# A hybrid decoder layer: one more weight block multiplied in seven products, and the gated DRAM transfers spread thinner over more jobs

## The chip, the cores and the metric

One core of a Trainium2 chip runs one launch of the kernel. The metric is the device time of that launch in microseconds (us); the lower, the better. Each kernel is executed several times, and the median is compared.

## The reference

One layer over 512 tokens (S) with a model width of 1024 (D), everything in float32:

```python
h = rmsnorm(x, norm_mix_g)
bg, cg, xv, q, k, v, z, a, b, ga, gb = split(h @ w_in)
y_a = (bg * causal_dwconv(cg * xv, conv_a_w)) @ w_a_out
y_b = gdn_branch(q, k, v, z, a, b, ...) @ w_b_out        # gated DeltaNet, 8 heads of 128
x = x + (sigmoid(ga) * y_a + sigmoid(gb) * y_b) @ w_o
h = rmsnorm(x, norm_ffn_g)
gate, val = split(causal_dwconv(h @ w_up, ffn_conv_w))   # 2 x 2816 columns
x = x + (silu(gate) * val) @ w_down
return rmsnorm(x, norm_final_g)
```

## The kernel before

**Jobs.** Every large matrix product is cut into jobs, and each job has one weight block of 1 MB: 16 tiles of 128x128, which make 256 output columns. `run_jobs` (L216) walks a list of 93 jobs. Job i's matmuls run while the block of job i+1 is split and the blocks of later jobs are loaded. The order is: jobs 0 to 15 make K, Q, V and Z of the DeltaNet branch; jobs 16 to 19 the gate GB; jobs 20 to 31 the convolution phase, four groups of CG, XV, BG; jobs 32 to 35 the gate GA; 36 to 39 `w_a_out` and 40 to 43 `w_b_out`; 44 to 50 `w_o`; 51 to 72 `w_up`; 73 to 92 `w_down`.

**Splitting.** A float32 weight is multiplied as a pair: `wh`, a rounded copy that ScalarE (ACT) makes at L150, and the rest `wl`, which VectorE (DVE) makes at L151. Three matmuls, wh by low part, wl by high part, wh by high part, stand for one exact product (`mm3`, L117). `wh` and `wl` have 12 buffers each (`WQ`). TensorE (PE) runs all of a job's matmuls from L109.

**Plain jobs and seven-product jobs.** A plain job (`col_job`, L249) splits 4 pieces and runs 48 matmuls of 512 columns. A seven-product job (`sum_job`, L308) uses a Strassen-like scheme over halves of the output columns, the depth and the tokens: 7 products of 12 matmuls of 256 columns, 84 matmuls in all. For that, its block (`SumBlock`, L165) makes sums of the weight quarters in place in the loaded buffer with four DVE instructions (L173), and splits 7 pieces instead of 4. The products run in the order 11, 12, s3, s2, s4, 22, s1. ACT copies partial results out of PSUM between them (`u` at L346 and L351, `v` at L349 and L353): product s2 writes the same PSUM bank that L346 reads, and so waits for it. Two DVE additions (L335, L339) then assemble the output, and the job's own use of it (`consume`) follows. In the convolution phase, all jobs but XV1 (job 24) are seven-product jobs. For them, half of `hT` is copied into a layout of its own (`hk`, `beside`, L305) by four transfers of POOL's DMA queue at the start of the phase.

**Loads.** There are two raw buffers. Block i+2 goes into the buffer of block i when the splits of block i are done. From job 21 on (`FINE`) a block is loaded in four quarters on SP's queue (L145, L206). Engines run ahead of PE: a load leaves as soon as its buffer is free.

**DRAM sums.** The products with `w_o` and `w_down` use sums of weight quarters too, made in DRAM by transfers on POOL's software queue: plain copies, and copies that add to what is there (`Sums.form`, L180, L1188). They are 112 transfers of 256 KB: first 32 for `w_o` (8 copies, 8 adding, 4 copies, 4 adding, 4 copies, 4 adding), then 80 for `w_down` in the same six steps (20, 20, 10, 10, 10, 10). They are handed out by `feed` (L235), which job i calls for block i+2: POOL copies one element of that block's raw buffer (the "gate copy", L237), which waits until the second quarter of the block has landed, and then issues the next few transfers. Gate copies and transfers are kept in program order on POOL. Everything else is ordered per engine by a scheduler at compile time, by readiness as it estimates it.

Before the change a gated job issues `FEED` = 3 transfers. The list is filled in `open_conv` (L1219), when job 20 starts, so the first gate copy is that of job 21. The `w_o` blocks (44 to 50) and the first two of `w_up` (51, 52) have no gate. The last of the 112 transfers goes out in job 67. `w_o`'s own sums are first loaded for job 44.

POOL also computes the small powers of the norms: `fac` (L1034) for the last heads of the DeltaNet branch, which ends in jobs 18 and 19, and `r` (L1450) in the norm ahead of `w_up`, which ends in jobs 48 to 50.

Of the kernel before, what the change touches and what calls it, by code (L numbers as in the profile page):

```python
# [26 lines left out]
C_BG, C_CG, C_XV, C_Q, C_K, C_V, C_Z, C_GA, C_GB = range(0, 36, 4)  # L27
# [2 lines left out]
Y_F = (5, 4, 6, 3)  # L30
WARM = 3
WQ = 12
FEED = 3
FINE = 21
Y_M = 10

# [25 lines left out]
def layer_kernel(ctx, tc, x, norm_mix_g, w_in, w_ab, conv_a_w, gdn_conv_w, gdn_A_log, gdn_dt_bias,  # L62
# [25 lines left out]
    def advance(queue, n):  # L88
        while n and queue:
            queue[0].step()  # L90
            if queue[0].done:
                queue.popleft()
            else:
                n -= 1
# [38 lines left out]
    class Block:  # L133
        def __init__(self, src, quarter=(4, P)):
            self.src, self.quarter = src, quarter
            self.raw, self.ready, self.lead, self.fed, self.fine = None, False, 2, True, False
            self.wh, self.wl = {}, {}

        def load(self):
# [55 lines left out]
    class FormBlock(Block):  # L195
        def __init__(self, runs, names, lead, place):
            super().__init__(None, (S,))
            self.runs, self.names, self.lead, self.place, self.fed = runs, names, lead, place, False

        def load(self):  # L200
            if self.raw is not None:
# [14 lines left out]
    def run_jobs(jobs):  # L216
        for block, _ in jobs[FINE:]:
            block.fine = True
        jobs[1][0].load()
        for i, (block, use) in enumerate(jobs):  # L220
            Task(block.split()).finish()
            drain(splits)
            if i + 1 < len(jobs):
                splits.append(Task(jobs[i + 1][0].split()))
            for j, (later, _) in enumerate(jobs[i + 2:i + 5]):
                if later.lead >= j + 2:
                    later.load()
            if adds and i + 2 < len(jobs) and jobs[i + 2][0].fed:
                feed(jobs[i + 2][0].raw)
            use(block.wh, block.wl)  # L230


    gate = const.tile([1, 64], F32, name="gate")

    def feed(raw):  # L235
        el = raw[0:1, 1]
        tc.keep_in_program_order(pool.tensor_copy(out=gate[:, 0:1], in_=el[:, 0:1]))  # L237
        advance(adds, FEED)


    def piece(w, j, k):
# [7 lines left out]
    def col_job(w, i, xs, consume, pre=None):  # L249
        def use(wh, wl):  # L250
            if pre:
                pre()
            x_ = xs() if callable(xs) else xs
            for j in range(GW // P):
                o = bank()
                products(o, wh, wl, j, x_)
                evacs.append(Task(consume(j, o)))
        return Block(lambda: w[i]), use
# [49 lines left out]
    def sum_job(w, i, xs, sums, consume, place, pre=None, uv=None, near=lambda: None):  # L308
        def use(wh, wl):
            if pre:  # L310
                pre()
            drain(sums_of)
            x_, ts, low = xs() if callable(xs) else xs, sums(), near()
            A, B, C = bank(), bank(), bank()
            L, R = slice(0, HS), slice(HS, S)
            dst = place()
            u, v = uv() if uv else (scratch("u"), scratch("v"))

            def times(o, form, b, first):
                mm3(o, [(wh[form][:, k], wl[form][:, k], b[0][:, k], b[1][:, k]) for k in range(ND // 2)],  # L320
                    first, not first)

            def quarter(K, T):
                if K and low:
                    return [low[e][T] for e in range(2)]
                return [x_[e][:, K * 4:K * 4 + 4, T * HS:T * HS + HS] for e in range(2)]

            def t(i_):
                return [ts[e][i_] for e in range(2)]

            d = dst.rearrange("p (j t c) -> p t j c", j=2, t=2)
            pair = lambda a: a.rearrange("p (j c) -> p j c", j=2)

            def firsts():
                dve.tensor_tensor(out=d[:, 0], in0=pair(B), in1=pair(u), op=ALU.add)  # L335
                yield

            def seconds():
                dve.tensor_tensor(out=d[:, 1], in0=A[:, L].unsqueeze(1).broadcast_to([P, 2, HS]), in1=pair(v),  # L339
                                  op=ALU.add)  # L340
                yield
                for j in range(2):
                    yield from consume(j, dst[:, j * S:(j + 1) * S])

            times(A[:, L], "11", quarter(0, 0), True)
            act.copy(out=u[:, L], in_=A[:, L])  # L346
            times(B[:, L], "12", quarter(1, 0), True)
            times(B[:, R], "s3", t(2), False)
            act.copy(out=v[:, R], in_=B[:, R])  # L349
            times(A[:, L], "s2", t(1), False)  # L350
            act.copy(out=u[:, R], in_=A[:, L])  # L351
            times(C[:, L], "s4", quarter(1, 1), True)
            act.copy(out=v[:, L], in_=C[:, L])  # L353
            times(B[:, R], "22", t(3), False)
            evacs.append(Task(firsts()))
            times(A[:, L], "s1", t(0), False)
            evacs.append(Task(seconds()))
        return SumBlock(lambda: w[i]), use
# [751 lines left out]
    jobs = []  # L1110
# [12 lines left out]
    def gb_use(g):  # L1123
        def c(j, o):
            act.activation(out=gb()[:, 2 * g + j, :], in_=o, func=AF.Sigmoid)
            yield
        return c

    def gb_place(g):
        return lambda: gb()[:, 2 * g:2 * g + 2, :].rearrange("p k n -> p (k n)")  # L1130
# [18 lines left out]
    uv = lambda: cvs  # L1149
    for g in range(4):  # L1150
        if g == 0:
            jobs.append(col_job(w_in, C_GB + g, hT, gb_use(g)))
        else:
            jobs.append(sum_job(w_in, C_GB + g, hT, hsums, gb_use(g), gb_place(g), uv=uv))


    st = {}
# [46 lines left out]
            return [(0, LAST, self.last)], [("v4", e) for e in range(LAST)]  # L1204

    down_w = Sums("d", w_down, (0, 1, 2, 3, 4, 5, 7, 8, 9, 10))
    EIGHT = 6
    o_w = Sums("o", w_o, (0, 1, 2, 3))

    def open_conv():  # L1210
        drain(evacs)
        drain(chains)
        drain(mids)
        drain(backs)
        p2.close()
        sc = st["sc"] = p3.enter_context(tc.tile_pool(name="sc", bufs=1, side="right"))
        st["ya"] = Rows([by_columns(page(n, "ya")) for n in ("kq1", "CT")])
        room["pool"] = sc
        adds.extend((Task(o_w.form()), Task(down_w.form())))  # L1219
        st["near"] = beside(hT, [[by_columns(t, HS) for t in halves_of(page(n, "hk", F32R, UP))] for n in ("KU1", "AV1")])  # L1220

    def open_mix():
# [16 lines left out]
    def xv_c(g):  # L1239
        def c(j, o):  # L1240
            m = 2 * g + j
            u = held[g][:, j * S:(j + 1) * S]
            dve.tensor_tensor(out=u, in0=o, in1=u, op=ALU.mult)
            c_ = tmp("c", 2)
            yield from conv(c_, u, ca_w(m), 3)
            held["c", m] = c_
        return c
# [9 lines left out]
    for g in range(4):  # L1257
        jobs += [sum_job(w_in, C_CG + g, hT, hsums, nothing, cg_place(g), None if g else open_conv,
                         near=near if g else lambda: None),
                 sum_job(w_in, C_XV + g, hT, hsums, xv_c(g), pair_out, near=near) if g != 1 else  # L1260
                 col_job(w_in, C_XV + g, hT, xv_c(g)),
                 sum_job(w_in, C_BG + g, hT, hsums, bg_c(g), pair_out, near=near)]

    def ga_c(g):
# [234 lines left out]
    def o_top(q):  # L1499
        def use(wh, wl):  # L1500
            for tau in range(2):
                for i in range(2):
                    times_b(o_banks, *mix_b(2 * q + i), FORMS_T, tau, wh, wl, i, q + i == 0, q + i == 2)
                if q == 1:
                    fin1(tau, [o_banks["11"][tau], o_banks["22"][tau]])
        return use
# [4 lines left out]
    jobs += [(FormBlock(*o_w.first_pass(p), 2, raw), o_first(p)) for p in range(ND // 2)]  # L1511
    jobs.append((FormBlock(*o_w.low(), 2, raw), o_low))
    jobs += [(FormBlock(*o_w.top(q), 2, raw), o_top(q)) for q in range(2)]


    gates = {}
# [72 lines left out]
    for g in range(NF // 2):  # L1589
        def up_job(i, c, plain, pre=None):  # L1590
            if plain:
                return col_job(w_up, i, lambda: st["h2"], c, pre)
            return sum_job(w_up, i, lambda: st["h2"], hsums, c, pair_out, pre,
                           near=near if 2 < i < NA // 2 + 1 or NF // 2 <= i < NF // 2 + NA // 2 else lambda: None)

        last = g == NF // 2 - 1
        gj = up_job(g, gate_c(g), g < 2 or last, (lambda: splits.append(prep_d(prep_a, 0))) if last else
                    start_near if g == 2 else None)
        vj = up_job(NF // 2 + g, val_c(g), g not in (4, 7))
        gj[0].fed = vj[0].fed = g > 0  # L1600
        jobs += [(gj[0], first_gate), (vj[0], first_val)] if g == 0 else [gj, vj]


# [216 lines left out]
```

## Time and profile before

| what | value |
|---|---|
| median of 3 executions | 948.6 us (947.57, 948.6, 950.33) |
| the profiled execution | 950.23 us |
| its span, first to last instruction | 948.5 us |
| mean granted TensorE clock | 0.996 |
| instructions | 17675 |
| gate copies on POOL (L237) | 38 |
| bytes read from and written to HBM | 133.64 MB, 32.78 MB |

The sums below are made against the profiled execution. "Busy" rows give the time in which an engine works and what share of the span that is; a row of a window "A:B" gives the same for the stretch from A to B us, with the number of instructions behind x, the granted clock, the busy share of the DMA engines and GB/s. A row of a group gives line, engine, operation, tiles (out<-in), count, busy time, mean ns of one, and behind the second bar the idle time of the engine just before these instructions with what ended it.

### The profile page before, as it was taken

To read this page: it belongs to the slowest core of one execution; us is meant where nothing else is said; L and a number is where in the kernel's file an instruction comes from. 1 tells how busy PE (TensorE), PEld (TensorE's weight loads), DVE (VectorE), ACT (ScalarE), POOL (GpSimd) and SP (SyncE) were. 2 spreads that over 40 slices of the span, in tenths; PEclk is the share of its full clock that TensorE was granted. 3 is DMA by queue.
4 is the path that set the end of the run, shared out by engine and by line. 5 is a ranking of instruction groups with operands and counts; after the bars stand their busy time and mean duration, and the time that the engine had idled before them with its cause. 6 is when DMAs were issued, how large, how long until landed. Compare 5 with 4: busy or idle time off the path is not lost. (4 is left out here: it accounts for less than half of the span.)

```text
span 948.5 us, 17675 instructions
## 1 busy us (share of the span) xinstructions
PE 933.4 (98%) x6512; PEld 824.5 (87%) x6512; DVE 779.5 (82%) x1448; ACT 547.0 (58%) x1202; POOL 176.5 (19%) x288
## 2 busy tenths in 40 slices
PE   8999999999999999999999999999999989999996
PEld 7888887987889999999888888988899988888885
DVE  6978686898968998999653679999999979969885
ACT  7895756576565654555632346466575556556563
POOL 3330401304111122221322000322314110000000
PEclk9999999999999999999999999999999999999999
DMA  6443312223023677867988355667976765077332
GB/s 231 157 142 103 116 54 90 76 63 89 9 91 90 197 178 160 209 170 179 295 203 179 89 176 199 164 172 223 231 177 203 155 133 173 6 276 251 107 100 89
DMA packets 82903, 142.42 MB, mean 150 GB/s; under 512 B 24795, under 2 KB 29824, under 8 KB 80256
## 3 DMA queue, kind: packets, MB, share of 16 engines
q1 hardware_dynamic: 65904, 107.47, 35.0%
q0 software_dynamic: 16768, 33.56, 18.2%
q8 instruction: 51, 0.84, 0.4%
q14 instruction: 36, 0.29, 0.1%
q10 hardware_dynamic: 144, 0.26, 0.1%
HBM read 133.64 MB, written 32.78 MB: 175 GB/s over the span
## 5 line engine op out<-in xcount | busy, mean ns | idle before, releaser
L150 ACT CAST wh<-raw 128x512 fp32r<-128x512 f32 x377 | 223.1, 620 | 189.6 <-PE ps L109 115.6
L151 DVE TENSOR_TENSOR wl<-raw,wh 128x512 fp32r<-128x512 f32 x377 | 250.7, 686 | 35.0 <-ACT wh L150 32.4
L109 PE MATMUL ps<-hT,wh 128*128 128x512 f32 (+1 forms) x888 | 251.7, 360 | 0.3 <-DVE hT L582 0.3
L109 PEld LDWEIGHTS ps<-hT,wh 128*128 128x128 f32 x888 | 156.9, 189 | 20.7 <-DVE hT L582 0.5
L109 PE MATMUL ps<-hT,wl 128*128 128x512 f32 (+1 forms) x444 | 152.2, 353 | 0.0
L109 PE MATMUL ps<-h,wh 128*128 128x512 f32 (+1 forms) x592 | 150.5, 341 | 0.0
L109 PEld LDWEIGHTS ps<-h,wh 128*128 128x128 f32 x592 | 103.5, 190 | 12.5
L109 PE MATMUL ps<-ts,wh 128*128 128x256 f32 x544 | 101.0, 279 | 1.5 <-ACT u L346 1.5
L109 PE MATMUL ps<-wh,xs 128*128 128x512 f32 (+1 forms) x320 | 96.7, 384 | 0.0
L109 PE MATMUL ps<-h,wl 128*128 128x512 f32 (+1 forms) x296 | 96.2, 341 | 0.0
L109 PEld LDWEIGHTS ps<-hT,wl 128*128 128x128 f32 x444 | 83.8, 189 | 9.8
L109 PEld LDWEIGHTS ps<-ts,wh 128*128 128x128 f32 x544 | 85.1, 188 | 2.2 <-ACT u L346 1.9
L173 DVE TENSOR_TENSOR raw<-raw 128x512 f32<-128x512 f32 x108 | 74.2, 687 | 3.2 <-POOL gate L237 1.2
L109 PEld LDWEIGHTS ps<-wh,xs 128*128 128x128 f32 x320 | 59.6, 188 | 11.8
L109 PE MATMUL ps<-ts,wl 128*128 128x256 f32 x272 | 65.5, 277 | 0.0
L109 PE MATMUL ps<-us,wh 128*128 128x256 f32 x320 | 59.3, 280 | 2.7 <-ACT u L346 2.7
L109 PEld LDWEIGHTS ps<-h,wl 128*128 128x128 f32 x296 | 56.2, 190 | 6.3
L109 PE MATMUL ps<-wl,xs 128*128 128x512 f32 (+1 forms) x160 | 61.4, 384 | 0.0
L237 POOL COPY gate<-raw 1x1 f32<-1x1 f32 x38 | 20.8, 546 | 207.5 <-DMA raw<-in_w_in_dram 74.4
L375 DVE SCALAR_TENSOR_TENSOR ct<-ps,wA,ct 128x511 f32<-128x511 f32 (+2 forms) x72 | 53.2, 741 | 4.0 <-ACT ct L372 3.8
L150 ACT CAST wh<-raws 128x512 fp32r<-128x512 f32 x66 | 39.5, 620 | 25.7 <-PE ps L109 8.6
L109 PEld LDWEIGHTS ps<-us,wh 128*128 128x128 f32 x320 | 50.7, 191 | 2.9 <-ACT u L346 2.9
(346 smaller groups left out, 1787.0 us busy)
## 6 DMA issues: line engine op xcount, KB each, us to landing
raw<-in_w_up_dram SPq DMA_DIRECT2D x88, 256.0 KB, 4.9
raw<-in_w_in_dram SPq DMA_DIRECT2D x20, 1024.0 KB, 5.2
raw<-in_w_in_dram SPq DMA_DIRECT2D x64, 256.0 KB, 4.7
dv<-in_w_down_dram POOLq DMA_DIRECT2D x50, 256.0 KB, 6.3
raws<-in_w_down_dram SPq DMA_DIRECT2D x32, 256.0 KB, 4.2
raws<-dv SPq DMA_DIRECT2D x24, 256.0 KB, 5.3
ov<-in_w_o_dram POOLq DMA_DIRECT2D x20, 256.0 KB, 6.1
raw<-in_w_a_out_dram SPq DMA_DIRECT2D x16, 256.0 KB, 5.7
```

The costliest lines, as they stand in the source:

```text
L109: pe.matmul(o, lhsT=a, rhs=b, start=start, stop=stop, skip_group_check=free)
L150: act.copy(out=wh, in_=src)
L151: dve.tensor_tensor(out=wl, in0=src, in1=wh.bitcast(F32), op=ALU.subtract)
L173: dve.tensor_tensor(out=r[q], in0=a, in1=b, op=op)
L237: tc.keep_in_program_order(pool.tensor_copy(out=gate[:, 0:1], in_=el[:, 0:1]))
L375: dve.scalar_tensor_tensor(out=dst[:, sh:], in0=src[:, :S - sh], scalar=wcol(j), in1=dst[:, sh:], op0=ALU.mult, op1=ALU.add)
```

## The change

1. XV1, the last plain job of the convolution phase (job 24), becomes a seven-product job like its neighbours.
2. A gated job issues two transfers (`FEED` = 2) instead of three. The 15 jobs whose blocks are 36 to 50 (`w_a_out`, `w_b_out`, `w_o`) get three (`FEED_MORE`); so the seven blocks of `w_o`, which had no gate, now have one.
3. The list is filled at the start of job 17 (GB1) instead of job 20 (CG0), so that jobs 18, 19 and 20 issue transfers too.

Counted out in the order of the jobs: jobs 18 to 33 issue 2 each (32, just the sums of `w_o`), jobs 34 to 48 issue 3 each (45), jobs 49 and 50 none, jobs 51 to 67 issue 2 each (34) and job 68 the last one. That is 49 gate copies instead of 38. The transfers themselves, their number, bytes and order, are the same.

```diff
-FEED = 3
+FEED = 2
+FEED_MORE = 3
...
-            self.raw, self.ready, self.lead, self.fed, self.fine = None, False, 2, True, False
+            self.raw, self.ready, self.lead, self.fed, self.fine = None, False, 2, FEED, False
...
-            self.runs, self.names, self.lead, self.place, self.fed = runs, names, lead, place, False
+            self.runs, self.names, self.lead, self.place, self.fed = runs, names, lead, place, 0
...
             if adds and i + 2 < len(jobs) and jobs[i + 2][0].fed:
-                feed(jobs[i + 2][0].raw)
+                feed(jobs[i + 2][0].raw, jobs[i + 2][0].fed)
...
-    def feed(raw):
+    def feed(raw, n):
         el = raw[0:1, 1]
         tc.keep_in_program_order(pool.tensor_copy(out=gate[:, 0:1], in_=el[:, 0:1]))
-        advance(adds, FEED)
+        advance(adds, n)
...
-            jobs.append(sum_job(w_in, C_GB + g, hT, hsums, gb_use(g), gb_place(g), uv=uv))
+            jobs.append(sum_job(w_in, C_GB + g, hT, hsums, gb_use(g), gb_place(g), (lambda: start_adds()) if g == 1 else None, uv=uv))
...
+    def start_adds():
+        adds.extend((Task(o_w.form()), Task(down_w.form())))
...
-        adds.extend((Task(o_w.form()), Task(down_w.form())))
...
-                 sum_job(w_in, C_XV + g, hT, hsums, xv_c(g), pair_out, near=near) if g != 1 else
-                 col_job(w_in, C_XV + g, hT, xv_c(g)),
+                 sum_job(w_in, C_XV + g, hT, hsums, xv_c(g), pair_out, near=near),
...
+    for block, _ in jobs[-15:]:
+        block.fed = FEED_MORE
...
-        gj[0].fed = vj[0].fed = g > 0
+        if g == 0:
+            gj[0].fed = vj[0].fed = 0
```

## The prediction

> **What bounds the kernel now.** I read the page's busy times first.
>
> ```profile
> PE 933.4 (98%) x6512; PEld 824.5 (87%) x6512; DVE 779.5 (82%) x1448; ACT 547.0 (58%) x1202; POOL 176.5 (19%) x288
> ```
>
> PE is the bound over the whole span, so an edit gains only by taking matmul time away or by closing one of PE's few pauses, and loses by opening one. Next come windows cut where jobs begin on PE: XV1, BG1, XV2, BG3, GA0, GA1, GA2.
>
> ```profile
> 351.90:362.80 10.90, 10.90 (x51) 9.02 (x50) 9.56 (x17) 3.91 (x8) 1.86 (x4) 1.00 0.94 221
> 362.80:372.40 9.60, 9.60 (x86) 9.60 (x84) 8.00 (x13) 5.72 (x12) 2.19 (x3) 1.00 0.84 158
> ...
> 382.00:391.60 9.60, 9.60 (x87) 9.60 (x85) 8.95 (x15) 5.03 (x11) 2.44 (x4) 1.00 0.66 216
> ...
> 420.40:430.00 9.60, 9.60 (x87) 9.60 (x85) 9.50 (x16) 4.24 (x10) 2.60 (x4) 1.00 0.70 170
> 430.00:440.00 10.00, 10.00 (x87) 9.86 (x86) 9.75 (x16) 5.13 (x11) 1.80 (x4) 1.00 0.72 195
> 440.00:450.60 10.60, 10.20 (x86) 9.99 (x85) 10.17 (x17) 8.02 (x18) 2.07 (x4) 1.00 0.65 176
> 450.60:461.70 11.10, 10.04 (x86) 9.85 (x85) 5.99 (x11) 8.24 (x19) 4.06 (x8) 1.00 0.94 306
> ```
>
> The columns are PE, PEld, DVE, ACT, POOL. A plain job takes 10.90 us, a seven-product job 9.60. DVE has 8.0 of 9.6 us to do right after the plain job, 9.5 by BG3: it falls behind over a row of seven-product jobs. By GA0 to GA2 PE needs 10.0, 10.6 and 11.1 us for a 9.6 us job: 2.9 us lost. The waits of that stretch (430 to 462 us) name the link:
>
> ```profile
> PEld ps L109 <- ACT u L346: 1.9, 2, 1.3
> ...
> ACT mixa L1266 <- DVE mixa L339: 0.8, 1, 0.8
> ```
>
> PE waits for the copy `u`, which stands in ACT's queue behind work that waits for DVE. That is the way a late DVE reaches PE.
>
> The last view is the chain that ended last, with windows around it (end of val 7, then gate 8 of `w_up`, job 67, from 767.0 to 781.4).
>
> ```profile
> 758.31 0.60 DVE o L339
> 758.91 0.60 DVE raw L173
> 759.51 0.60 DVE wl L151
> ...
> 763.36 0.61 DVE raw L173
> 763.97 0.02 SPq L145
> 764.00 0.03 issue
> 764.03 8.50 DMA raw<-in_w_up_dram
> ...
> 772.60 0.62 ACT wh L150
> 773.22 0.62 ACT v L372
> 773.84 0.27 ACT u L346
> ```
>
> ```profile
> 757.30:767.00 9.70, 9.70 (x86) 9.70 (x85) 8.96 (x15) 7.58 (x16) 2.71 (x4) 1.00 0.69 94
> 767.00:776.90 9.90, 7.20 (x51) 7.00 (x51) 5.54 (x10) 3.64 (x7) 1.01 (x2) 0.86 0.77 216
> 776.90:781.40 4.50, 4.50 (x38) 4.50 (x38) 4.43 (x8) 1.09 (x4) 0.00 (x0) 0.93 0.40 27
> ```
>
> Job 67 takes 14.4 us instead of 9.6: 4.8 us lost in one place, the largest pause of the run. A quarter of a later block was loaded in 8.50 us; ACT, in order, waited for it with the copy `u` of job 67 behind. `u` ended at 774.1. PE could have used it after three of its seven products, at 767.0 + 3/7 x 9.6 = 771.1, so 3.0 us are the pause. The clock rows (0.86 over 9.9 us, 0.93 over 4.5 us) give 1.4 + 0.3 = 1.7 us of lost clock: together 4.7.
>
> Why was the load slow? The median quarter of this weight takes 4.9 us, and three adding transfers were under way:
>
> ```profile
> raw<-in_w_up_dram SPq DMA_DIRECT2D x88, 256.0 KB, 4.9
> ```
>
> ```profile
> 758.05 2.54 POOL L1188 DMA_DIRECT2D dl<-in_w_down_dram  x3 [0.37 <-issue]
> ```
>
> ```profile
> DMA to landing us min/median/max: 7.3/9.2/11.3
> ```
>
> The last row is that of these three alone. Issued about 0.5 us apart from 758.05, they land near 765.4, 767.8 and 770.4, one every 2.5 us. The load, issued at 764.03, shared the DMA engines with two of them.
>
> **The change part by part.**
>
> *XV1 in seven products.* PE: 10.90 to 9.60, a gain of 1.3 us. DVE gets three more L151, four L173, one L335 and one L339: nine instructions at 0.60 us (the chain shows all three kinds at that spacing), 5.4 us. With the job 1.3 us shorter DVE stands 6.7 us later against PE. ACT gets three casts and four copies at about 0.6 and 0.4 us, 3.4 us, and has room (3.91 of 10.90 busy). What covers the 6.7 us is DVE's idle time from XV1 to GA0, of which these groups have all that counts:
>
> ```profile
> L151 DVE TENSOR_TENSOR wl<-raw,wh 128x512 fp32r<-128x512 f32 x58 | 38.6, 687 | 4.3 <-ACT wh L150 3.4
> L173 DVE TENSOR_TENSOR raw<-raw 128x512 f32<-128x512 f32 x33 | 22.7, 688 | 0.7
> ...
> L1243 DVE TENSOR_TENSOR o<-ps,o 128x512 f32<-128x512 f32 x2 | 1.4, 688 | 1.1 <-PE ps L109 1.1
> ```
>
> That is 4.3 + 0.7 + 1.1 = 6.1 us in 351.9 to 440. Most of the first figure is DVE waiting for a cast that ACT could not make because PE still held the `wh` buffers; a later DVE no longer waits for that. If all of it fills, 0.6 us are left over; some turn-around from L173 to cast to L151 stays, so I take 1.2 us. It comes out at GA1, where no slack is left. XV1 nets -1.3 + 1.2 = -0.1 us. Ends: -1.3 (no pause grows) and -1.3 + 6.7 = +5.4 (no idle time fills).
>
> *Earlier start: six copies in jobs 18 to 20.* POOL's queue there:
>
> ```profile
> 299.99 0.78 POOL L305 DMA_DIRECT2D hk<-hT  x1 [3.71 <-issue]
> 301.41 2.03 POOL L1034 TENSOR_TENSOR fac<-fac,nhalf 128x8 f32<-128x8 f32 x1 [0.64 <-DVE fac L1033]
> 309.59 0.78 POOL L305 DMA_DIRECT2D hk<-hT  x1 [6.15 <-PE ps L765]
> 316.37 0.76 POOL L305 DMA_DIRECT2D hk<-hT  x1 [6.00 <-issue]
> 324.17 0.18 POOL L237 COPY gate<-raw 1x1 f32<-1x1 f32 x1 [7.04 <-DVE raw L173]
> 324.71 1.64 POOL L1188 DMA_DIRECT2D ov<-in_w_o_dram  x3 [0.37 <-issue]
> ```
>
> A gate copy with two copies takes 0.18 + 0.37 + 2 x 0.55 = 1.6 us of POOL. The scheduler already moved `hk` ahead of `fac`, so it may do so with job 19's gate. Then `fac` starts at 300.8 + 1.6 + 0.2 = 302.6 instead of 301.4, and behind it wait, in turn, DVE's scaling by `fac`, L339 of GB2, ACT's sigmoid and the copy `u` of GB3:
>
> ```profile
> 305.85 0.35 ACT L346 COPY ct<-ps 128x256 f32<-128x256 f32 x1
> ```
>
> ```profile
> 302.50:313.20 10.70, 10.70 (x95) 10.70 (x94) 9.61 (x22) 6.18 (x13) 1.72 (x2) 1.00 0.36 100
> ```
>
> The copy ends at 306.2. The window is GB3's, so PE needs it after three of seven products, at 302.5 + 4.1 = 306.6. So 1.2 - 0.4 = 0.8 us if the gate goes first, 0 if not; I take 0.3. `hk` costs nothing: XV0 begins three jobs of 9.6 us before XV1, at 323.1, and reads the quarter that the last transfer brings in its fifth product, at 328.6; issued at 316.4 + 1.6 and even 6.0 us in flight (the wait behind the one before), it is there at 324.8. The cover is gone if the gate's own load comes over 3.8 us late, and then it costs what is late.
>
> *Two instead of three in jobs 21 to 33 and 51 to 66.* In the first stretch PE waits for no load, so this gains nothing. In the second it takes the third adding transfer out of the pile-up ahead of job 67. If the engines serve one thing after another, the load lands 2.5 us sooner, at 770.0, and 1.6 us of ACT work later PE has `u` at 771.6: a pause of 0.5. If load and transfers share half and half, it lands 1.25 sooner and the pause is 1.8. Nearer to the first: landings 2.5 us apart look like one after the other. I take 0.6 and no lost clock: 4.7 to 0.6, a gain of 4.1. Ends: 4.7 and 0 (the load comes late anyway). The Trainium skill ("DMA: Bandwidth & Descriptors", Queues, rings and completion order) says that each DMA engine goes round between the queues that have work, packet by packet; by that the pause of 1.8 would be right. No row here shows the turns.
>
> *Three each for `w_o`, 21 transfers in jobs 42 to 48.* POOL has been idle for long when the norm's power comes:
>
> ```profile
> 589.96 0.86 POOL L1450 TENSOR_TENSOR r<-r,nhalf 128x1 f32<-128x1 f32 x1 [77.41 <-ACT hn L1446]
> ```
>
> Loads run ahead of PE, and the last of these blocks is split before 587; with its gate at some 580 and 2.5 us for three transfers POOL is free 7 us early. Cost 0; without that cover up to 2.5 us, on the way to `w_up`. A wait of DVE for a gate copy (L173 rewrites what it reads) costs nothing either while DVE is ahead.
>
> *Last transfers in jobs 67 and 68.* Three late ones instead of one: 0, or job 67's pause again one job on.
>
> Sum on the profiled execution: 950.2 - 0.1 + 0.3 - 4.1 = 946.3. It was 1.6 us above the median of its three runs. No run shows whether the median one has the pause in full; I take half: 946.3 - 0.8 = 945.5.
>
> **Rivals.**
>
> (1) *The pause stays, or moves.* ACT's order is fixed before the run, and a cast needed 20 us later still stands ahead of `u`. For it: eight quarters and the transfers crowd together whatever the third does. Against it: the load needs to be only 3 us faster, and 4.9 is usual. Median 948.6 - 0.1 + 0.3 = 948.8.
>
> (2) *Shared engines*: load and transfers halve the engines, the pause is 1.8 instead of 0.6, 946.7. For it, the three transfers and the load were all slower than the median load. The skill's rule above is this one.
>
> (3) *XV1's gain is kept*: DVE's idle time fills wholly and GA1 is reordered, 945.5 - 1.2 = 944.3. For it, 6.1 of 6.7 us are there; against it, GA1 waits for DVE already.
>
> (4) *DVE becomes the bound of the convolution phase* (the slower end). At BG3 it is 99% busy already. If little of the idle time fills, `u` comes 6.7 us late at GA0 or GA1 instead of 1.2, 5.5 more; and a pause of some 3 us cost 1.7 of clock at 774, so 945.5 + 5.5 + 1.7 = 952.7. It decides once 5.5 of the 6.7 us reach GA1 as a pause (5.5 - 1.2 + 1.7 = 6.0 above the forecast). Against it: BG1's 1.6 us idle are the first to fill. The Trainium skill ("TensorE: Matmul & The Clock Gate", HAM oscillation) says that the clock falls to half when PE idles beyond about 3.4 us; job 67's rows, 0.86 after a pause of 3.0 us, agree roughly.
>
> (5) *POOL's queue ahead of CG0*: `fac` and `hk` both late by 2 us or so: 2.8 us at GB3 or XV0 instead of 0.3, 945.5 + 2.5 = 948.0. For it, POOL is in order and `hk` waits for the one before; against it, the covers of 0.4 and 3.8 us above.
>
> **How the numbers follow.** Forecast 0.40, (1) 0.20, (2) 0.08, (3) 0.15, (4) 0.14, (5) 0.03. The time is the likeliest's, 945.5. About 0.3% (2.85 us) is what a measurement tells from no change, so "faster" is below 945.8 and "slower" above 951.5. The forecast's own range is 943.5 to 947.5 and gives 0.23 to faster and 0.17 to same. With (3) and 0.02 of (2) faster has 0.40; with (1), (5), 0.06 of (2) and 0.02 of (4) same has 0.48; the rest of (4) is slower, 0.12. The range goes from 942.5 (rival 3 with the run-to-run spread of some 2 us below it) to 950.0 (rival 1 with 1.2 above it). It leaves out (4) and a little of the best end, 0.2 together.
>
> **What would show it.** Right: XV1's window at 9.6 us; DVE near 9.5 busy from BG1 on and GA1 some 1.2 us longer; job 67 near 10 us with clock 1.00; no load of 8.5 us in the chain; POOL's `fac` within 1.2 us of DVE's L1033. Wrong: GA0 to GA2 together beyond 36 us (DVE is the bound), a pause of 3 us anywhere in `w_up`, or waits of L1450 or `hk` behind L1188.

## The result: the changed kernel is slower

The changed kernel takes 956.23 us at the median (955.06 to 956.67), the kernel before 947.83 us in the same series (946.7 to 950.33): a ratio of 1.0083, 95% interval 1.0069 to 1.0097. The forecast was 945.5 us. In the profiled execution the span grew from 948.5 to 954.9 us, 6.4 us. That of before was a slow one of its series, so the medians lie further apart, by 8.4 us. Line numbers named here are one higher in the changed kernel from L109 on, two to three higher from L1243 on.

The windows of the profile after answer to those shown of before: XV1, CG2, XV2, GA0, GA1, GA2, then the whole o phase (first `w_o` product to first `w_up` product) in three pieces, then job 67. The columns are PE, PEld, DVE, ACT, POOL, granted clock, DMA share, GB/s.

```profile
352.30:361.90 9.60, 9.60 (x87) 9.60 (x86) 9.26 (x16) 5.98 (x14) 2.21 (x3) 1.00 0.59 141
...
371.50:381.50 10.00, 9.89 (x87) 9.69 (x86) 9.76 (x16) 5.14 (x11) 1.75 (x3) 1.00 0.58 165
381.50:392.00 10.50, 9.81 (x86) 9.61 (x85) 10.07 (x17) 6.78 (x16) 1.53 (x3) 1.00 0.57 181
...
432.20:442.30 10.10, 10.00 (x86) 9.80 (x85) 9.85 (x16) 5.23 (x12) 2.13 (x3) 1.00 0.54 118
442.30:452.90 10.60, 10.20 (x87) 10.00 (x86) 10.17 (x17) 8.03 (x18) 2.25 (x3) 1.00 0.68 155
452.90:466.80 13.90, 11.48 (x86) 11.29 (x85) 7.67 (x13) 9.65 (x21) 4.07 (x8) 0.88 0.96 286
...
564.80:588.00 23.20, 22.59 (x100) 18.41 (x99) 19.58 (x29) 15.30 (x25) 6.48 (x11) 1.00 0.94 280
588.00:600.90 12.90, 9.85 (x44) 7.78 (x42) 11.86 (x21) 6.62 (x16) 1.57 (x3) 1.00 0.74 240
600.90:610.60 9.70, 9.64 (x44) 8.11 (x44) 8.20 (x15) 5.51 (x13) 0.93 (x1) 0.82 0.35 113
...
778.10:787.90 9.80, 9.80 (x87) 9.80 (x86) 9.73 (x17) 4.75 (x11) 3.32 (x5) 1.00 0.93 206
```

XV1 takes 9.6 us, as forecast. Job 67 takes 9.8 us at full clock, so its pause is gone, as forecast. But CG2, XV2, others of the jobs up to GA0, and GA2 above all are longer than before (GA2 13.9 us with a clock of 0.88; before 11.1). And the o phase is 23.2 + 12.9 + 9.7 = 45.8 us long; before it was 40.1. By phase, from first matmul to first matmul:

| phase | before | after | difference |
|---|---|---|---|
| start of GB1 | 272.2 | 272.6 | +0.4 |
| GB1 to the end of GA3 | 200.5 | 205.2 | +4.7 |
| `w_a_out`, `w_b_out` | 87.0 | 87.0 | 0 |
| o phase | 40.1 | 45.8 | +5.7 |
| `w_up` | 234.9 | 230.6 | -4.3 |
| `w_down` and the end | same | same | 0 |

PE's waits from CG2 to GA2 (375 to 470 us) name the copies `u` and `v`, and those of ACT from XV1 to GA2 (352 to 470 us) show what holds the copies up:

```profile
PE ps L110 <- ACT u L347: 2.8, 2, 2.4
PE ps L110 <- ACT v L350: 1.4, 2, 0.7
```

```profile
ACT wh L151 <- DVE raw L174: 35.9, 24, 3.2
...
ACT wh L151 <- DMA raw<-in_w_a_out_dram: 3.6, 1, 3.6
```

ACT's casts wait for DVE's weight sums, and the copies `u` and `v`, for which PE waits, stand behind the casts. The second of ACT's rows is GA2's. ACT's timeline there, and then PE's:

```profile
457.70 0.62 ACT L151 CAST wh<-raw 128x512 fp32r<-128x512 f32 x1 [3.61 <-DMA raw<-in_w_a_out_dram]
458.22 1.14 ACT L1268 ACTIVATE mixa<-mixa 128x512 f32<-128x512 f32 x2
459.27 0.35 ACT L347 COPY u<-ps 128x256 f32<-128x256 f32 x1
```

```profile
459.68 0.39 PE L110 MATMUL ps<-ts,wh 128*128 128x256 f32 x1 [2.42 <-ACT u L347]
```

A cast for a block needed later waits 3.61 us for its load, two activations and `u` stand behind it, PE waits 2.42 us, and the clock falls.

The o phase is read in the chain of work that ended last, cut to 575 to 612 us:

```profile
568.20 13.63 DMA raw<-ol
...
586.68 10.11 DMA raw<-in_w_up_dram
...
596.89 0.62 ACT wh L151
597.51 0.63 ACT hn L1448 x2
...
599.17 0.86 POOL r L1452
...
600.06 0.76 DVE hn L1454
...
600.96 1.05 PE ps L1463 x4
```

The load of the last quarters of `ol` (the low block of `w_o`, block 48) takes 13.63 us. So everything behind it is late: the splits, then the release of the next buffer, so that a quarter of `w_up` is loaded at 586.68, again slowly. A cast waits for that quarter with the norm's `hn` behind it, then come POOL's power `r` and the second `hn`. PE waits 3.12 us, until 600.96, and then runs at half clock (0.50 from 601 to 604 us; 0.82 over 9.7 us is 1.7 us lost). The transfers of 565 to 585 us, KB each and median us from issue to landing, and then the row of the same load before:

```profile
x<-in_x_dram SPq DMA_DIRECT2D x4, 512.0 KB
...
dv<-in_w_down_dram POOLq DMA_DIRECT2D x4, 256.0 KB, 10.8
...
raw<-ol SPq DMA_DIRECT2D x2, 256.0 KB, 13.7
```

```profile
raw<-ol SPq DMA_DIRECT2D x2, 256.0 KB, 8.0
```

The gate of block 48 opens at 566.4 us, just as the four loads of `x` (2 MB) leave for the norm (from 566.1 on), and the last two quarters of `ol` come behind these on the same queue.

### The profile page after: what moved, and what is told of

It reads as the page before. It is cut to its first block, busy times and chain, and to the rows that moved or that the text cites. A ratio compares the mean times of both kernels' runs of the same rounds, so it can differ in the third digit from the quotient of the medians.

```text
span 954.9 us, 17798 instructions
## 1 busy us (share of the span) xinstructions
PE 935.6 (98%) x6548; PEld 826.8 (87%) x6548; DVE 785.4 (82%) x1457; ACT 548.7 (57%) x1209; POOL 178.5 (19%) x299
## 4 chain that ended last, share of the span: by engine, by line
PE 80%; DVE 9%; ACT 4%; DMA 3%; issue 3%; POOL 1%; POOLq 0%; ACTq 0%; DVEq 0%
PE ps L110 72%; DVE raw L174 2%; DVE wl L152 2%; ACT wh L151 2%; DMA raw<-ol 1%; PE ps L801 1%; PE ps L766 1%; DMA raw<-in_w_up_dram 1%; DVE c L376 1%; DMA raw<-in_w_a_out_dram 1%; PE ps L548 1%; PE ps L1024 1%; PE ps L1004 1%; DVE o L340 1%; PE ps L1013 0%
## 5 line engine op out<-in xcount | busy, mean ns | idle before, releaser
L151 ACT CAST wh<-raw 128x512 fp32r<-128x512 f32 x380 | 224.7, 620 | 191.2 <-PE ps L110 95.0
L152 DVE TENSOR_TENSOR wl<-raw,wh 128x512 fp32r<-128x512 f32 x380 | 254.3, 688 | 38.8 <-ACT wh L151 35.7
L110 PE MATMUL ps<-hT,wh 128*128 128x512 f32 (+1 forms) x864 | 244.5, 360 | 0.3 <-DVE hT L583 0.3
L110 PEld LDWEIGHTS ps<-hT,wh 128*128 128x128 f32 x864 | 153.2, 190 | 19.4 <-DVE hT L583 0.5
L110 PE MATMUL ps<-hT,wl 128*128 128x512 f32 (+1 forms) x432 | 147.6, 352 | 0.0
L110 PE MATMUL ps<-ts,wh 128*128 128x256 f32 x576 | 108.0, 281 | 4.8 <-ACT u L347 2.8
L110 PEld LDWEIGHTS ps<-ts,wh 128*128 128x128 f32 x576 | 90.5, 189 | 6.3 <-ACT u L347 3.2
L174 DVE TENSOR_TENSOR raw<-raw 128x512 f32<-128x512 f32 x112 | 77.0, 687 | 2.2
L110 PEld LDWEIGHTS ps<-wh,xs 128*128 128x128 f32 x320 | 59.6, 188 | 11.8
L110 PE MATMUL ps<-ts,wl 128*128 128x256 f32 x288 | 69.6, 278 | 0.0
L110 PEld LDWEIGHTS ps<-ts,wl 128*128 128x128 f32 x288 | 54.4, 189 | 0.0
L151 ACT CAST wh<-raws 128x512 fp32r<-128x512 f32 x66 | 39.7, 620 | 25.6 <-PE ps L110 8.4
```

Source lines behind the costliest of these rows:

```text
L110: pe.matmul(o, lhsT=a, rhs=b, start=start, stop=stop, skip_group_check=free)
L151: act.copy(out=wh, in_=src)
L152: dve.tensor_tensor(out=wl, in0=src, in1=wh.bitcast(F32), op=ALU.subtract)
L174: dve.tensor_tensor(out=r[q], in0=a, in1=b, op=op)
```

## The experiments

Two losses are to be explained, each with a rival. In the convolution phase, A: VectorE has more work than the jobs are long; B: the adding transfers cost the time. In the o phase, C: the three transfers ahead of block 48; D: the sum of all new gates. First each half of the change by itself, the change without the one gate, and a first feeding without any gate in `w_o`.

**xv1_alone**: the kernel before with

```diff
-                 sum_job(w_in, C_XV + g, hT, hsums, xv_c(g), pair_out, near=near) if g != 1 else
-                 col_job(w_in, C_XV + g, hT, xv_c(g)),
+                 sum_job(w_in, C_XV + g, hT, hsums, xv_c(g), pair_out, near=near),
```

> The kernel before with XV1 in seven products and nothing else. Theory A (DVE is the bound of the convolution phase: it has about 9.5 us of work in each 9.6 us job, so the time that XV1 takes from PE and gives to DVE comes back as pauses at CG2 to GA2): XV1 takes 9.6 us, GB1's start to GA3's end takes about 205 instead of 200.5 us, the median is about 947.8 + 4.7 = 952.5 us. Rival B (the phase lost its time to the two adding transfers per job that start three jobs sooner): this phase stays at 199 to 200.5 us and the median at 946.5 to 948 us. The pause of job 67 and the o phase (40.1 us from the first w_o product to the first w_up product) stay as before under both.

Measured 950.39 us, ratio 1.0036 (1.0022 to 1.0050). GB1 to GA3 takes 202.9 us. The groups CG2 to BG2 and CG3 to BG3, 28.8 us each before:

```profile
371.70:401.80 30.10, 29.34 (x255) 28.95 (x254) 29.32 (x48) 16.17 (x35) 9.21 (x14) 1.00 0.81 192
401.80:432.20 30.40, 29.38 (x255) 28.98 (x254) 29.62 (x49) 16.46 (x36) 6.89 (x12) 1.00 0.73 180
```

DVE is busy for 29.3 and 29.6 us of these (48 and 49 instructions), more than the 28.8 that three jobs need on PE. So XV1 costs time by itself. The rest of the 4.7 us needs the new feeding as well: GA2 is 11.8 us here and 13.9 there.

**feeding_alone**: the changed kernel with XV1 plain again.

> The changed kernel with XV1 plain again: only the feeding of the adding transfers is changed. Theory A: GB1 to GA3 takes 200.5 us as before; the o phase takes about 45.8 us as in the changed kernel (+5.7, theory C: three adding transfers ahead of block 48 share the DMA engines with the loads of x and of the last w_o blocks); job 67's pause is gone (-2 to -4.3). Median 947.8 + 5.7 - (2 to 4.3) = 949 to 951.5 us. Rival B: GB1 to GA3 stays at about 205 us, median 954 to 956 us.

Measured 952.56 us, ratio 1.0055 (1.0041 to 1.0069): the o phase 45.1 us, GB1 to GA3 201.0, `w_up` 231.7, job 67 9.8. Rival B falls as far as CG2 to GA0 go: those jobs are as before. Only GA2 is longer, 11.8 us for 11.1. The median lies 1 us above what was expected; the profile has two new pauses of some 0.4 us each in `w_up`, which may be why.

**no_gate_48**: the changed kernel with

```diff
     for block, _ in jobs[-15:]:
         block.fed = FEED_MORE
+    jobs[-3][0].fed = 0
```

> The changed kernel without the gate and the three adding transfers ahead of block 48 (the w_o block of the low halves); they move to the end of the list, two each. Theory C (these three, issued at 567 us beside four loads of x, delay the loads of blocks 48 to 51): the w_o quarters land in 7 to 8 us instead of 13, the o phase takes 40 to 42 us instead of 45.8, median 956.2 - (4 to 5.7) = 950.5 to 952.2 us. Rival D (it is the sum of all transfers of that phase, the six copies at 585 us among them, or the later rows of x): the o phase stays above 44 us, median 955 to 956.5 us.

Measured 951.94 us, ratio 1.0053 (1.0038 to 1.0068). The o phase falls from 45.8 to 40.5 us, though the other six gates are still there. The load:

```profile
raw<-ol SPq DMA_DIRECT2D x2, 256.0 KB, 8.9
```

**plain_no_wo**: feeding_alone (so XV1 is plain) with three transfers for each of the blocks 20 to 43, none in `w_o`, two for each of the last 20 of `w_up`.

```diff
-    for block, _ in jobs[-15:]:
-        block.fed = FEED_MORE
+    for block, _ in jobs[20:44]:
+        block.fed = FEED_MORE
+    for block, _ in jobs[44:]:
+        block.fed = 0
```

> XV1 plain, the list begun at GB1 as in the changed kernel, three transfers for each of the blocks 20 to 43, none for the seven w_o blocks and w_up's first two, two for each of the last twenty w_up blocks: 72 + 40 = 112 transfers, the whole list. Theories A and C: GB1 to GA3 200.5 us, o phase 40.1 us, job 67's pause gone: median 947.8 - (2 to 4.3) = 943.5 to 946 us. If three transfers per job from GB1 on cost time in the convolution phase it shows there: above 202 us, median 946 to 949 us.

Measured 948.2 us, ratio 1.0012 (0.9999 to 1.0025): no gain. The o phase is 40.1 and job 67 9.8, but three transfers each from GB1 on make CG1 10.9 us long (9.6 before) and GA2 12.2. And job 57 (gate 3 of `w_up`) takes 13.3 us instead of 9.6: transfers and the `hk` copies meet its loads. Taking a crowd away in one place had put it in another. (Its profiled execution, 951.91 us, was the slowest of twelve, so the median has less of these losses.)

**spread**: feeding_alone again, with the transfers where the runs had shown room. In `w_up` the first group and groups 2 and 3 (blocks 51, 52, 55 to 58) have none.

```diff
-    for block, _ in jobs[-15:]:
-        block.fed = FEED_MORE
+    for k, n in [(range(20, 51), 0), (range(23, 35), 3), (range(36, 44), 4), (range(44, 48), 3)]:
+        for i in k:
+            jobs[i][0].fed = n
...
-        if g == 0:
+        if g in (0, 2, 3):
             gj[0].fed = vj[0].fed = 0
```

> XV1 plain, and the 112 adding transfers where the runs so far showed room: from CG0 on three for each of the blocks 23 to 34, none for block 35 (its three share the DMA engines with the first load of w_a_out, for which GA2 waits 1.20 us in the kernel before), four each for the eight blocks of w_a_out and w_b_out, three each for w_o's four first blocks, none for the low and top blocks of w_o, none for the first two groups of w_up nor for the two blocks fetched while the hk halves are copied, two each for the other sixteen w_up blocks. If every loss is a load that meets adding transfers (theory E): GA2 falls from 11.1 to 9.9 to 10.4 us, the o phase stays at 40.1 to 40.5, w_up at 230 to 231 with no pause over 0.6 us; median 947.8 - 2 to 4 = 944 to 946 us. If GA2's wait is for the buffer and not for the transfers (theory F), GA2 stays at 11 us; if the four each for w_a_out and w_b_out are too many, these two phases exceed 43.5 us each.

Measured 944.43 us, ratio 0.9963 (0.9950 to 0.9976): faster than both kernels. GA2 (450 to 460 us) and job 67:

```profile
450.30:460.10 9.80, 9.80 (x86) 9.77 (x85) 5.93 (x11) 8.38 (x19) 4.84 (x10) 1.00 0.92 282
765.40:775.20 9.80, 9.80 (x87) 9.80 (x86) 9.73 (x17) 4.78 (x11) 6.56 (x6) 1.00 0.85 202
```

No job of `w_up` has a pause, `w_a_out` and `w_b_out` stay at 43.5 us each with four transfers a job, the o phase is 40.1. For GA2 its trace decides between theories E and F. GA2's cast waits for the second quarter of `w_a_out`'s first block. That quarter leaves 2.0 us ahead of GA2 in spread as in feeding_alone (at 448.3 and 448.4 us), so the buffer comes free as early. But it lands after 3.4 us in spread, where no transfer is let go ahead of block 35, and after 6.6 us in feeding_alone, where two are. The wait is for the load and not for the buffer: theory E.

**before_again**: the kernel before, for a second profile.

> The kernel before once more, for its profile: how large job 67's pause is in another execution. The prediction's sum went by the one profiled execution with 4.7 us, which was the slowest of six; at the median of 947.8 us, 2.4 us below it, the pause would be about 2 to 3 us (w_up 232.5 instead of 234.9 us) with the other phases within 0.4 us of the first profile.

Its span is 944.7 us. GA2 and job 67:

```profile
450.70:460.70 10.00, 10.00 (x86) 9.90 (x86) 6.15 (x11) 8.41 (x19) 4.06 (x8) 1.00 1.04 343
766.40:777.50 11.10, 10.31 (x86) 9.91 (x85) 9.30 (x16) 4.52 (x10) 1.01 (x2) 1.00 0.81 192
```

Job 67 takes 11.1 us here and 14.4 in the first profile; GA2 10.0 and 11.1. The kernel before has loads that arrive just in time or just too late, from one execution to the next. So at job 67 there were 1.3 us to gain in this execution and 4.6 in the first, and GA2 can be 10 us long with block 35's transfers under way (the quarter for which its cast waits took 4.7 us here and 6.0 in the first profile).

**xv1_no_taps**: xv1_alone without the two taps behind each XV job.

```diff
-            yield from conv(c_, u, ca_w(m), 3)
+            act.activation(out=c_, in_=u, func=AF.Copy, scale=ca_w(m)(2))
+            yield
+            yield
```

> XV1 in seven products as in xv1_alone, and the two taps of the convolution behind each XV job left out (four VectorE instructions less in each group of three jobs; the output is not the reference's). Theory A (VectorE is the bound once it has 9.5 us in each 9.6 us job): the waits at CG2, XV2, CG3, XV3 and GA0 vanish, XV1 keeps its 1.3 us, GB1 to GA3 takes 198 to 199.5 us instead of 202.9. Rival G (ACT's queue order alone makes `u` and `v` late, whatever VectorE has to do): jobs of 10.0 to 10.6 us remain and the phase stays above 201.5 us.

Measured 944.34 us; GB1 to GA3 takes 196.6 us. The same two groups:

```profile
370.60:399.40 28.80, 28.80 (x254) 28.80 (x253) 26.97 (x44) 16.58 (x35) 7.74 (x12) 1.00 0.90 209
399.40:428.20 28.80, 28.80 (x254) 28.80 (x253) 26.97 (x44) 16.58 (x35) 7.19 (x12) 1.00 0.69 177
```

PE has no pause left, and XV1 keeps its 1.3 us. ACT's waits in 352 to 440 us turn round; first this kernel, then xv1_alone:

```profile
ACT wh L150 <- PE ps L109: 28.7, 10, 3.2
ACT wh L150 <- DVE raw L173: 9.2, 15, 1.5
```

```profile
ACT wh L150 <- DVE raw L173: 30.7, 19, 3.2
```

With less for VectorE to do, ACT waits for PE to give buffers back; with XV1 in seven products and the taps, it waits for VectorE. That is what theory A said. Rival G isn't fully excluded by this run, for the scheduler ordered ACT's work anew too (in CG2 three casts stand between `v` of L349 and `u` of L351 here, and one in xv1_alone). What speaks for theory A besides is the count of VectorE's work further down.

**xv1_pool**: xv1_alone with BG's multiplication on GpSimd.

```diff
-            dve.tensor_tensor(out=st["ya"][:, m, :], in0=o, in1=held.pop(("c", m)), op=ALU.mult)
+            pool.tensor_tensor(out=st["ya"][:, m, :], in0=o, in1=held.pop(("c", m)), op=ALU.mult)
```

> XV1 in seven products as in xv1_alone, and the multiplication by the convolved rows behind each BG job (two 128x512 instructions per group) on GpSimd instead of VectorE. Theory A: 1.2 to 1.4 us of VectorE's work per group go, about what a group is over 28.8 us; the waits at CG2 to XV3 shrink to under 0.3 us each and GB1 to GA3 takes 199.5 to 201 us, median 947 to 948.5 us instead of 950.4. If GpSimd slows VectorE while both work, or the gates and adding transfers queued behind the multiplications come late, the phase stays at 202 us or more.

Measured 958.0 us, ratio 1.0102 (1.0077 to 1.0128); GB1 to GA3 213.4 us, a clear loss. POOL's and DVE's timelines at CG1:

```profile
347.73 1.65 POOL L1252 TENSOR_TENSOR ya<-o,c 128x512 f32<-128x512 f32 x1
```

```profile
346.11 4.55 DVE L173 TENSOR_TENSOR raw<-raw 128x512 f32<-128x512 f32 x3
```

Three instructions of 0.69 us took 4.55 us: the one that met the multiplication did not end before it. The Trainium skill ("SBUF — State Buffer", SBUF: two separate sides) says that the two engines' shared port is held by one instruction as a whole while the other engine's blocks. The trace agrees as far as that one instruction took 3.10 us, from 346.84 to 349.94, and so outlasted the multiplication (347.73 to 349.38); by the recorded starts it had begun first. The run says nothing against theory A, but this way out is closed. How much of the loss comes from such meetings, and how much from gates and transfers that stand behind the multiplications on POOL, was not measured.

The last kernels measure the size of each loss.

**gate_48_alone** and **gate_48_one**: the feeding of the kernel before, and three transfers, or one, also ahead of block 48.

```diff
+    jobs[48][0].fed = True
```

This is the edit with three.

> The kernel before with one edit: three adding transfers also ahead of block 48 (the low block of w_o), so that the list ends one w_up job earlier. Theory C (these three are enough by themselves to make the loads of the next w_o and w_up blocks late): o phase 44 to 46 us instead of 40.1, median 947.5 + 4 to 5.5 = 951.5 to 953 us. Rival D (they hurt only together with the gates of the other six w_o blocks): o phase 40 to 41.5 us, median 946.5 to 949 us.

> As gate_48_alone, with one adding transfer ahead of block 48 instead of three. If the loss goes with what is in flight beside the loads, one transfer delays them by a third, about 2 us instead of 5.7, most of which the 2 to 3 us of lead that the loads have in the kernel before takes up: o phase 40.1 to 41.5 us, median 947 to 949 us. If it is a matter of the place alone (the gate's copy, or any transfer there), the o phase is above 43 us.

With three: 949.33 us, ratio 1.0017 (1.0002 to 1.0033). The o phase takes 44.2 us, +4.1, which is theory C; the median rose by less, and in its profile `w_up` takes 230.4 us, without the pause of job 67. With one: 946.65 us, ratio 0.9991 (0.9974 to 1.0008), o phase 40.1. Of each, the kinds of queue (packets, MB, share of 16 engines; q1 is SP's, q0 POOL's) in 15 us of the o phase and the load; three transfers first, then one:

```profile
q1 hardware_dynamic: 1142, 3.41, 65.2%
q0 software_dynamic: 432, 0.79, 31.2%
...
raw<-ol SPq DMA_DIRECT2D x2, 256.0 KB, 12.2
```

```profile
q1 hardware_dynamic: 1730, 4.47, 83.9%
q0 software_dynamic: 144, 0.26, 10.7%
...
raw<-ol SPq DMA_DIRECT2D x2, 256.0 KB, 9.5
```

The load takes 8.0 us with no transfer beside it (8.9 in no_gate_48), 9.5 with one, 12.2 with three: 1.1 to 1.4 us for each of the three. One costs nothing, so the o phase has at least 1.5 us to spare; three cost a pause of 2.5 us and 1.7 us of clock (0.87 over 13.0 us):

```profile
590.00:603.00 13.00, 10.50 (x48) 8.52 (x47) 11.40 (x22) 8.19 (x19) 1.79 (x2) 0.87 0.37 121
```

**spread_xv1**: spread with XV1 in seven products.

> The kernel named spread with XV1 in seven products: what that edit costs where no load is late. Theory A: XV1 takes 9.6 us, the jobs from CG2 to GA0 lose 0.4 to 1.0 us each at five or six places, GB1 to GA3 takes 200 to 201.5 us instead of 199.05, median 944.4 + 1 to 2.5 = 945.4 to 947 us. Rival H (the loss in the convolution phase was late loads, not VectorE): 197.8 to 199 us, median 943 to 944.4 us.

Measured 947.25 us, ratio 0.9995 (0.9985 to 1.0005). GB1 to GA3 takes 201.6 us, 2.6 more than in spread; CG2 and XV2 are 10.0 and 10.6 us as in xv1_alone. That is XV1's price where no load is late; rival H falls.

## Why the prediction was wrong

*Three each for `w_o`: the term of 0 measured +5.7 us, the largest failure.* The step looked at one cover only, POOL's time before the norm's power. It never asked what the DMA engines had to do at block 48: four loads of `x`, then the quarters of `w_o` and `w_up`, from which ACT, `hn`, POOL's `r` and PE follow. no_gate_48 gives back 5.3 of the 5.7 us, and gate_48_alone takes 4.1 by itself; the other 1.6 us come only together with the rest of the change. The prediction had the figure in its own rows: transfers landing 2.5 us apart and a load of 8.50 us beside them. It used this at job 67 and not here.

*XV1 in seven products: the term of -0.1 measured +2.6 us (spread_xv1).* The PE part, -1.3, was right. The lag was taken as 6.7 us, once, against 6.1 us of idle time that would fill. It fills only in part: in xv1_alone the same groups in the same stretch are left with 2.3 us of idle:

```profile
L151 DVE TENSOR_TENSOR wl<-raw,wh 128x512 fp32r<-128x512 f32 x61 | 40.4, 686 | 1.4
L173 DVE TENSOR_TENSOR raw<-raw 128x512 f32<-128x512 f32 x34 | 23.4, 688 | 0.9
```

So 6.1 - 2.3 = 3.8 us filled and 2.9 were left over, where 1.2 was taken. The jobs CG2 to GA0 are together 3.2 us longer than before. Behind that stands a count that the prediction didn't make. A group of three seven-product jobs gives VectorE 47 instructions (21 on L151, 12 on L173, 6 on L335 and L339, 4 taps, 4 multiplications). In the two rows of xv1_alone VectorE is busy for 58.9 us with 97 instructions, 0.61 us each, so 47 need 28.6 us, for 28.8 us of PE. That leaves 0.2 us for turn-around, and VectorE's idle time in these two groups was 0.8 us each. It is a loss in each such group. The plain XV1 had given VectorE a lead, and the two groups after it lived on that lead. Rival (4) named this mechanism, at 952.7 us; alone it gave 950.39. The test set for it, GA0 to GA2 beyond 36 us, did not fire (10.1 + 10.6 + 13.9 = 34.6), as the pauses lay mostly ahead of GA0.

*The feeding in the convolution phase: no term in the prediction.* The changed kernel loses 4.7 us there, of which XV1 is about 2.6. GA2 has most of the rest: 13.9 us with both halves of the change, 11.8 with either alone. Each half adds a little to its pause. The quarter of `w_a_out` for which the cast waits takes 6.0 us in the first profile of before, 6.1 in xv1_alone, 6.6 in feeding_alone and 6.7 in the changed kernel (3.4 in spread and 3.8 in spread_xv1, with no transfer ahead of block 35). And with XV1 in seven products two activations, 1.14 us together, stand between the cast and `u`; with XV1 plain it is one of 0.62 us. Together the pause reaches 2.42 us (1.06 before) and the clock drops for 0.12 x 13.9 = 1.7 us. This drop is what the two halves have in common and neither has alone.

*Two instead of three: -4.1 taken, -4.3 measured* on the profiled execution, where job 67's pause vanished as described. All thirteen profiles bear this step out: job 67 takes 9.7 to 9.8 us in the seven where job 66's gate lets one or two transfers go, and 10.0 to 14.4 us in the six where it lets three go. At the median the gain is smaller: before_again had only 1.3 us of that pause. The prediction allowed for this with 0.8 us; the two profiles of before differ by 2.8 us in `w_up`.

*Earlier start (+0.3 taken, 0 measured at its place) and last transfers (0)*: the jobs GB1 to XV0 are equal within 0.1 us, and jobs 67 and 68 have no pause. Rival (5) has nothing for it.

By measured terms, on the profiled execution: 950.2 + 0.4 (start of GB1) + 4.7 + 5.7 - 4.3 = 956.7 us; it took 956.67.

What stays open: how far ACT's order, beside VectorE's work, makes the jobs CG2 to GA0 longer; what makes up the 1.6 us of the o phase beyond gate_48_alone's 4.1; and why GA2's load took 6.0 us in one execution of before and 4.7 in the other, with the same three transfers let go ahead of it.

## What to carry to other kernels

Before work goes to an engine that is off the critical path, count its instructions per period against the period of the bound engine: idle time that is a lead left by one easier job is spent once and not in each period. Price a background transfer by the loads in flight at the very moment when it is let go, at each place where it is put, for moving it out of one crowd may put it into another. And when a pause of a few microseconds is at stake, add what the clock takes behind it.

## What the runs showed of the hardware

An adding transfer held the DMA engines about twice as long as a load of the same size. By the queue rows above, 31.2% for 0.79 MB against 65.2% for 3.41 MB is 39.5 against 19.1% per MB; with one transfer, 41.2 against 18.8. The shares may hold waiting too.

No fixed length of a pause decides on the clock. Here are a pause of 1.82 us (plain_no_wo, PE's timeline, then its window) that was followed by half clock, and one of 2.15 us (xv1_pool) that was not:

```profile
678.74 0.38 PE L110 MATMUL ps<-us,wh 128*128 128x256 f32 x1 [1.82 <-ACT v L350]
```

```profile
676.00:688.00 12.00, 10.18 (x55) 9.13 (x54) 10.55 (x17) 6.19 (x12) 3.68 (x6) 0.86 0.90 191
```

```profile
350.91 0.39 PE L109 MATMUL ps<-ts,wh 128*128 128x256 f32 x1 [2.15 <-ACT v L349]
```

```profile
346.00:360.00 14.00, 11.85 (x104) 11.65 (x103) 13.74 (x19) 6.28 (x13) 5.61 (x9) 1.00 0.64 136
```

The longer pauses of the convolution phase, the o phase and job 67 were all followed by a loss: 2.25 us (no_gate_48), 2.42 and 3.12 (the changed kernel), 2.45 (feeding_alone), 2.50 (gate_48_alone) and 2.70 (job 67 before, reckoned as 3.0 in the prediction) by one of about 1.7 us each, 2.86 (xv1_pool) by one of 3.4 us (0.66 over 10.0 us). The rule that the prediction cited from the Trainium skill ("TensorE: Matmul & The Clock Gate", HAM oscillation), a loss beyond about 3.4 us, is too lenient here by the measured rows.
